# A hybrid convolution trunk on one core: activations stored as even then odd tokens and read alternately by TensorE, with VectorE's background tasks in smaller portions

## The chip, the cores and the metric

The kernel runs on one core of one Trainium2 chip. The metric is the device time of one execution in microseconds. Three timed runs of the kernel before gave 2077.26, 2077.28 and 2077.67 us; the median is 2077.28 us. Engines are named as in the profile: PE is TensorE's matmuls, PEld its weight loads, DVE is VectorE, ACT is ScalarE, POOL is GpSimd and SP is SyncE, which issues nearly all DMAs.

## What is computed

One layer of a decoder trunk for 320 tokens, 256 of one prompt and 64 of eight sampled sequences with eight tokens each, in float32, with 2048 channels:

```python
h = rmsnorm(x) * norm_mix_g
b_a, c_a, v_a, glu_a, glu_b, gate_a, gate_b = split(h @ w_in)
y_a = (b_a * causal_dwconv3(c_a * v_a)) @ w_out_a
u   = glu_a * sigmoid(glu_b)
z   = silu(layernorm(causal_dwconv31(u) + bias))
y_b = z @ w_out_b
x   = x + (sigmoid(gate_a) * y_a + sigmoid(gate_b) * y_b) @ w_o
h2  = rmsnorm(x) * norm_ffn_g
x   = x + (silu(h2 @ w_gate) * (h2 @ w_up)) @ w_down
y   = rmsnorm(x) * final_norm_g
```

The inner width of the last pair of products is 5632. The two convolutions run along the tokens of each sequence, and for the sampled sequences they continue from a stored state.

## The kernel before

**Layout.** Activations lie transposed: channels on the 128 partitions and the 320 tokens along the free dimension, one tile of 128x320 for each block of 128 channels. The host has laid out `x` in this way, with the gains of the first norm in front of it.

**Products.** Each float32 product is made of three matmuls on numbers split into a high part (`float32r`) and the remainder: high weight by high activation (L221), high weight by low activation (L222), low weight by high activation (L223). The weights are the stationary operand, 128x128, and the 320 tokens are the moving operand, which is read from one tile in the order of the tokens. A unit is a product that gives 256 output channels (`begin`, `run`): two accumulators in PSUM, and for each of its 128-channel steps three matmuls for each accumulator. Its weights come in pieces of four steps: 512 KB loaded on SP's queue (L146, five buffers, four pieces ahead), then the high part is cast by ACT (L181) and the remainder is subtracted by DVE (L185), two pieces ahead, into one of three pairs of buffers. A full piece is 24 matmuls.

**Order of the work.** The first three units run as one group while `x` arrives. Then come the units of the gated unit's two halves (`post_gb`, `post_ga`), of the three-tap mixer (`post_c`, `post_v`, `post_b`), of gate a and `w_out_a`, of gate b, of `w_out_b`, of `w_o`, then two halves of gate, up and down. Each unit ends in its `post` function, where DVE and ACT read the accumulators. Where the result is the next product's activation, `hilo` (L267) splits it: an ACT copy gives the high part and a DVE subtraction the low part. The high and low parts of the tiles `a`, `z`, `m` and `f` come from there, those of `g` from L582 and L583.

**Background tasks.** The 31-tap convolution of mixer B, and the layernorm after it, are lists of small tasks in `bg`, mostly for DVE (a tap is L394). After each piece `pump` takes tasks off the list until their written costs reach a budget; what a task took too much is carried over as debt. A tap's written cost is 0.42, a channel's end 0.4. The budgets are 0.9 in the first three units after the group, `BG1` = 1.3 for the ten units of the gated unit's rest (40 pieces), `BG2` = 1.3 for the 24 units of the three-tap mixer (96 pieces), and `BG3` = 1.1 for the units of the two gates and `w_out_a` (96 pieces). What is left is run at once before the units of `w_out_b`. The whole program passes through a scheduler that may move instructions within an engine's queue.

**The end.** The last 256 output channels of the last product are computed with tokens as rows (`run_rows`): there the activations are the stationary operand and 256 columns of weights the moving one, in 176 matmuls. Three blocks of tokens (`blk`: two of 128 of the prompt, one of the 64 sampled) are finished in turn by `Out`, which scales the rows, multiplies the tiles `xg` by the spread factors and writes them out. The norm's sums come from `row_sums`, as PE transposes of `facc`.

**Twenty matmuls more.** After the last block's DMAs have been put in the queue (L764 to L774), 20 matmuls write an accumulator that nobody reads. All have the same stationary tile. In order: four read a tile `v` of 128x320 in its order, four read it as `v.rearrange("p (a b) -> p b a", a=2)`, which takes word 0, word 160, word 1, word 161 and so on, four read 316 of its words from the third on, four read one word 320 times, and four read the same bytes as bfloat16.

Of the kernel before, what the change touches and what calls it, by code (L numbers as in the profile page):

```python
# [8 lines left out]
F32 = mybir.dt.float32  # L9
F32R = mybir.dt.float32r  # L10
I32 = mybir.dt.int32
AF = mybir.ActivationFunctionType
# [26 lines left out]
def trunk_kernel(ctx: ExitStack, tc: tile.TileContext, a):  # L39
# [22 lines left out]

    blk = [(0, P), (P, P), (2 * P, TS)]
    HD = D // 2
# [5 lines left out]
    gmix, xc[0] = lead[:, 0:NC], lead[:, NC : NC + T]  # L70
    sp.dma_start(out=lead, in_=a["x"][:, 0 : NC + T])

    def xcol(c):
        return a["x"][:, NC + c * T : NC + (c + 1) * T]

    def load_x(cs):
        for c in cs:
            xc[c] = slot("xc")
            sp.dma_start(out=xc[c], in_=xcol(c))  # L79

# [130 lines left out]
    def begin(u):  # L211
        acc = [ps_acc.tile([P, 512], F32, tag="acc", name=nm("acc")) for _ in range(u["nj"])]
        hi, lo = u["acts"]()
        nk = u["nk"]

        def prod(q, k, j):
            kk = q["ka"] + k
            wh = q["hi"][:, k, j * P : (j + 1) * P]
            wl = q["lo"][:, k, j * P : (j + 1) * P]
            o = acc[j][:, :T]  # L220
            te.matmul(o, wh, hi[kk], start=(kk == 0), stop=False)  # L221
            te.matmul(o, wh, lo[kk], start=False, stop=False)  # L222
            return te.matmul(o, wl, hi[kk], start=False, stop=(kk == nk - 1)).ins  # L223

        return acc, prod
# [64 lines left out]

    def sums(p, **kw):

        te.matmul(p[:, :T], ones_r, s_hi, start=True, stop=False)
        return te.matmul(p[:, :T], ones_r, s_lo, start=False, stop=True).ins

# [33 lines left out]
    def x_factor():  # L329
        p = pst("rps")  # L330
        halves(lnacc)
        with tc.issue_after(last_mm[0]):
            last_mm[0] = sums(p)
# [6 lines left out]
        ve.scalar_tensor_tensor(out=rb, in0=lnt, scalar=1.5, in1=rb, op0=ALU.add, op1=ALU.mult)  # L340

    def x_norm(c):
        hr = slot("hr")
        ve.scalar_tensor_tensor(out=hr, in0=xc[c], scalar=g_mix(c), in1=rb, op0=ALU.mult, op1=ALU.mult)
        h_hi[c], h_lo[c] = hilo(hr, "h")

# [225 lines left out]
    def post_o(b):  # L572
        def f(acc):
            for j in range(2):
                c = 2 * b + j
                xr = slot("xr")
                nc.sync.dma_start(out=xr, in_=xcol(c))
# [43 lines left out]
    def post_d1(b):  # L621
        def f(acc):
            for j in range(2):
                c = 2 * b + j
                ve.tensor_tensor(out=x2[c], in0=acc[j][:, :T], in1=x2[c], op=ALU.add)
        return f
# [36 lines left out]
    def pack(k):  # L663

        if k % 2 == 0:
            pk.append(slot("pk", F32R))
        t = pk[k // 2]
        ac.copy(out=t[:, (k % 2) * P : (k % 2) * P + TS], in_=f_hi[HF + k][:, TP:T])
        ac.copy(out=t[:, (k % 2) * P + TS : (k % 2 + 1) * P], in_=f_lo[HF + k][:, TP:T])

    def end_prep(n):

        if n == 0:
            t = slot("gfin", shape=(P, NB))
            nc.sync.dma_start(out=t, in_=a["final_norm_g"][CT * P : D].partition_broadcast(P))
            ve.tensor_scalar(out=t, in0=t, scalar1=-0.5, scalar2=None, op0=ALU.mult)
            gfin.append(t)
            for c in (CT, CT + 1):
                z = slot("xz", shape=(P, P))
                nc.gpsimd.memset(z[:, TS:P], 0.0)  # L680
                ac.copy(out=z[:, 0:TS], in_=x2[c][:, TP:T])
                xz.append(z)

    def run_rows(u):
        acc = [ps_acc.tile([P, 512], F32, tag="acc", name=nm("acc")) for _ in range(3)]

        def block(i, q, ks=None):
            for k in ks or range(q["n"]):
                kk = q["ka"] + k
                h, l, o = f_hi[HF + kk], f_lo[HF + kk], acc[i][:, :NB]  # L690
                wh, wl = q["hi"][:, k, :], q["lo"][:, k, :]
                t0 = blk[i][0]
# [69 lines left out]
        B.part(4, CB)  # L762


        o = ps_acc.tile([P, 512], F32, tag="acc", name=nm("acc"))
        w, v = f_hi[HF][:, 0:P], f_hi[HF + 1]
        wb, vb = f_hi[HF][:, 0 : P // 2].bitcast(mybir.dt.bfloat16), f_hi[HF + 1].bitcast(mybir.dt.bfloat16)
        with tc.issue_after(last_mm[0]):
            for rhs in (v, v.rearrange("p (a b) -> p b a", a=2), v[:, 2:318], v[:, 0:1].broadcast_to((P, T))):
                for _ in range(4):  # L770
                    r = o[:, : rhs.free_size()]
                    last_mm[0] = te.matmul(r, w, rhs, start=True, stop=True, skip_group_check=True).ins  # L772
            for _ in range(4):
                last_mm[0] = te.matmul(o[:, :T], wb, vb[:, 0:T], start=True, stop=True, skip_group_check=True).ins  # L774
    def row_sums():
        p = pst("pv")
        for i, (t0, n) in enumerate(blk):
            last_mm[0] = te.matmul(
                p[:n, i * P : (i + 1) * P], facc[:, t0 : t0 + n], ident, is_transpose=True, start=(i == 0), stop=True,
                skip_group_check=True,  # L780
            ).ins
# [8 lines left out]
    class Out:  # L790
# [77 lines left out]
        def part(self, c0, c1, eng=nc.sync):  # L868
            n, w = self.n, 1024 // self.n
            while c0 < c1:  # L870
                h = c0 * n // 1024
                e = min(c1, 12 if c0 < 12 else CT, (h + 1) * w)
                if self.out[h] is None:
                    self.out[h] = wp.tile([P, KP * NB], F32, tag="raw", bufs=RAW_BUFS, name=nm("yo"))
                o = self.out[h][:, (c0 - h * w) * n : (e - h * w) * n]
                t, k = (xgt[0], c0) if c0 < 12 else (xgt[1], c0 - 12)
                v = t[:, k * T : (k + e - c0) * T].rearrange("p (c t) -> p c t", t=T)[:, :, self.t0 : self.t0 + n]
                self.dve(
                    ve.tensor_tensor, out=o.rearrange("p (c t) -> p c t", t=n), in0=v,
                    in1=self.rb.unsqueeze(1).broadcast_to((P, e - c0, n)), op=ALU.mult,  # L880
                )
                eng.dma_start(out=self.dst[1][:, c0:e, :], in_=o)
# [51 lines left out]

    BG1, BG2, BG3 = 1.3, 1.3, 1.1
    first_units = group([
# [91 lines left out]


def _lay_in(np, i):  # L1030

# [5 lines left out]
    x = np.concatenate([f["x_prompt"].reshape(TP, D), f["x_sample"].reshape(TS, D)])  # L1037
    o["x"] = np.concatenate([_rows(np, f["norm_mix_g"]).reshape(P, NC), _rows(np, x).reshape(P, NC * T)], axis=1)
    names = ("final_norm_g", "norm_ffn_g", "conv_b_bias", "ln_b_g", "ln_b_b", "conv_a_w", "conv_b_w")
# [9 lines left out]
def _lay_out(np, y):  # L1049
    def rows(v, n):  # L1050
# [9 lines left out]
    return (  # L1060
        np.concatenate(yb[:2])[None],
        yb[2].reshape(SB, SS, D),
        np.ascontiguousarray(na[: WA - 1])[None, None],
# [24 lines left out]
```

## Time and profile before

| quantity | value |
|---|---|
| median of three timed runs | 2077.28 us |
| time of the profiled execution | 2076.96 us |
| its span, first to last instruction | 2075.2 us |
| PE busy, matmuls | 2069.2 us, 14117 |
| DVE busy | 1268.7 us (61%) |
| ACT busy | 807.7 us (39%) |
| DMA moved | 321.17 MB, 155 GB/s on average |
| granted TensorE clock | 1.000 |

The profiled execution lies 0.32 us under the median of the timed runs, and its own time 1.8 us over its span. Busy PE is no proof of a PE at its best, because matmuls are pipelined and their ends are modelled: a matmul of 320 columns shows 309 ns, though 14117 of them share 2069.2 us, 147 ns each. What counts is the distance from start to start. An engine's share over the whole span is an average of stages that differ, so the stages are read one by one.

### The profile page before, as it was taken

To read this page: it belongs to the slowest core of one execution; us is meant where nothing else is said; L and a number is where in the kernel's file an instruction comes from. 1 tells how busy PE (TensorE), PEld (TensorE's weight loads), DVE (VectorE), ACT (ScalarE), POOL (GpSimd) and SP (SyncE) were. 2 spreads that over 40 slices of the span, in tenths; PEclk is the share of its full clock that TensorE was granted. 3 is DMA by queue.
4 is the path that set the end of the run, shared out by engine and by line. 5 is a ranking of instruction groups with operands and counts; after the bars stand their busy time and mean duration, and the time that the engine had idled before them with its cause. 6 is when DMAs were issued, how large, how long until landed. Compare 5 with 4: busy or idle time off the path is not lost.

```text
span 2075.2 us, 33945 instructions
## 1 busy us (share of the span) xinstructions
PE 2069.2 (100%) x14117; PEld 2066.8 (100%) x14117; DVE 1268.7 (61%) x1854; ACT 807.7 (39%) x1172; POOL 4.5 (0%) x26
## 2 busy tenths in 40 slices
PE   9999999999999999999999999999999999999999
PEld 9999999999999999999999999999999999999999
DVE  7898889988986754345555645445334545545445
ACT  6544344444434344333344333333323333333433
POOL 0000000000000000000000000000000000000000
PEclk9999999999999999999999999999999999999999
DMA  7555544444444444444455444444455444444553
GB/s 268 156 171 156 181 145 153 153 149 147 155 153 145 150 153 149 148 151 153 151 174 173 152 146 150 153 150 141 146 159 152 148 151 153 148 148 147 150 153 112
DMA packets 97906, 321.17 MB, mean 155 GB/s; under 512 B 12920, under 2 KB 20920, under 8 KB 97720
## 3 DMA queue, kind: packets, MB, share of 16 engines
q1 hardware_dynamic: 97320, 318.48, 49.5%
q8 instruction: 110, 1.80, 0.4%
q10 hardware_dynamic: 432, 0.52, 0.1%
q14 instruction: 44, 0.36, 0.1%
HBM read 315.42 MB, written 4.98 MB: 154 GB/s over the span
## 4 chain that ended last, share of the span: by engine, by line
PE 99%; DMA 1%; DVE 0%; SPq 0%; ACT 0%; issue 0%
PE acc L223 33%; PE acc L221 33%; PE acc L222 33%; DMA raw<-in_w_in 1%; PE acc L695 0%; PE acc L696 0%; PE acc L697 0%; PE acc L700 0%; PE acc L701 0%; PE acc L772 0%; DVE yo L808 0%; DVE rl L320 0%; DVE wlo L185 0%; SPq L146 0%; SPq L79 0%; PE acc L708 0%
## 5 line engine op out<-in xcount | busy, mean ns | idle before, releaser
L185 DVE TENSOR_TENSOR wlo<-raw,whi 128x1024 fp32r<-128x1024 f32 (+1 forms) x602 | 717.3, 1192 | 706.5 <-ACT whi L181 703.5
L181 ACT CAST whi<-raw 128x1024 fp32r<-128x1024 f32 (+2 forms) x601 | 615.9, 1025 | 1177.6 <-PE acc L222 927.6
L222 PE MATMUL acc<-hl,whi 128*128 128x320 f32 x1600 | 494.2, 309 | 0.0
L221 PE MATMUL acc<-hh,whi 128*128 128x320 f32 x1600 | 493.8, 309 | 0.0
L223 PE MATMUL acc<-hh,wlo 128*128 128x320 f32 x1600 | 493.4, 309 | 0.0
L223 PE MATMUL acc<-gh,wlo 128*128 128x320 f32 x1408 | 435.1, 309 | 0.0
L222 PE MATMUL acc<-gl,whi 128*128 128x320 f32 x1408 | 435.1, 309 | 0.0
L221 PE MATMUL acc<-gh,whi 128*128 128x320 f32 x1408 | 435.1, 309 | 0.0
L222 PEld LDWEIGHTS acc<-hl,whi 128*128 128x128 f32 x1600 | 300.4, 188 | 0.0
L221 PEld LDWEIGHTS acc<-hh,whi 128*128 128x128 f32 x1600 | 300.3, 188 | 0.0
L223 PEld LDWEIGHTS acc<-hh,wlo 128*128 128x128 f32 x1600 | 300.2, 188 | 0.0
L221 PEld LDWEIGHTS acc<-gh,whi 128*128 128x128 f32 x1408 | 264.3, 188 | 0.0
L223 PEld LDWEIGHTS acc<-gh,wlo 128*128 128x128 f32 x1408 | 264.3, 188 | 0.0
L222 PEld LDWEIGHTS acc<-gl,whi 128*128 128x128 f32 x1408 | 264.3, 188 | 0.0
L394 DVE SCALAR_TENSOR_TENSOR cb<-win,prm,cb 128x320 f32<-128x320 f32 x480 | 257.2, 548 | 7.4
L221 PE MATMUL acc<-fh,whi 128*128 128x320 f32 x660 | 203.9, 309 | 0.0
L222 PE MATMUL acc<-fl,whi 128*128 128x320 f32 x660 | 203.9, 309 | 0.0
L223 PE MATMUL acc<-fh,wlo 128*128 128x320 f32 x660 | 203.9, 309 | 0.0
L222 PEld LDWEIGHTS acc<-fl,whi 128*128 128x128 f32 x660 | 123.9, 188 | 0.0
L223 PEld LDWEIGHTS acc<-fh,wlo 128*128 128x128 f32 x660 | 123.9, 188 | 0.0
L221 PEld LDWEIGHTS acc<-fh,whi 128*128 128x128 f32 x660 | 123.9, 188 | 0.0
L221 PE MATMUL acc<-ah,whi 128*128 128x320 f32 x256 | 79.1, 309 | 0.0
(183 smaller groups left out, 2039.2 us busy)
## 6 DMA issues: line engine op xcount, KB each, us to landing
raw<-in_w_in SPq DMA_DIRECT2D x221, 512.0 KB, 3.6
raw<-in_w_gate SPq DMA_DIRECT2D x88, 512.0 KB, 3.6
raw<-in_w_up SPq DMA_DIRECT2D x88, 512.0 KB, 3.6
raw<-in_w_down SPq DMA_DIRECT2D x80, 512.0 KB, 3.6
raw<-in_w_out_a SPq DMA_DIRECT2D x32, 512.0 KB, 3.6
raw<-in_w_out_b SPq DMA_DIRECT2D x32, 512.0 KB, 3.6
raw<-in_w_o SPq DMA_DIRECT2D x32, 512.0 KB, 3.7
raw<-in_w_down SPq DMA_DIRECT2D x16, 256.0 KB, 2.7
```

The costliest lines, as they stand in the source:

```text
L181: return f(out=q["hi"][:, ks, :], in_=q["raw"][:, ks, :]).ins
L185: return ve.tensor_tensor(out=q["lo"][:, ks, :], in0=q["raw"][:, ks, :], in1=q["hi"][:, ks, :].bitcast(F32), op=ALU.subtract).ins
L221: te.matmul(o, wh, hi[kk], start=(kk == 0), stop=False)
L222: te.matmul(o, wh, lo[kk], start=False, stop=False)
L223: return te.matmul(o, wl, hi[kk], start=False, stop=(kk == nk - 1)).ins
L394: ve.scalar_tensor_tensor(out=o, in0=win[0][:, :, j + 2 : j + 10], scalar=w_cb(j, c), in1=o, op0=ALU.mult, op1=ALU.add)
```

## The change

Tiles that PE streams are stored in halves: first the 160 even tokens, then the 160 odd ones. PE reads them with the pattern "p (a b) -> p b a", that is, one word from the first half and one from the second in turn, so the products come out in the order of the tokens as before. `alt` names this view of a stored tile, `seq2` the matching view of a tile in the order of tokens.

- `begin`: all three matmuls of each product read `alt(hi)` and `alt(lo)`.
- `hilo`, `post_o`, and the residual of the last product (`post_d2`, and `post_d1` for the last two channel blocks) write `alt` views from `seq2` views: on DVE and ACT the stored side then hops 160 words with each word. In the instructions these tiles stand as 128x160x2.
- The host stores a copy of `x` in halves (`xs`), which the first stage uses, so that `x_norm` stays in the stored order; it needs the norm's factors in that order as well, a copy `rbh` made once. `post_o` still loads `x` in the order of tokens.
- `run_rows`: the 256 weight columns of the last block of `w_down` are stored in halves by the host for its second half of rows, and read alternately. The blocks of tokens become even prompt tokens, odd prompt tokens and the sampled ones, which now are two runs of 32 in a tile (`smp`, `two`); the host puts the tokens of the output in order. `row_sums` first collects the sampled tokens' sums in a tile `fs` by an ACT copy.
- The 20 matmuls at the end are gone.
- `BG1` and `BG2` are 1.1 for 1.3, `BG3` is 1.25 for 1.1.

```diff
-    blk = [(0, P), (P, P), (2 * P, TS)]
+    HT = T // 2
+    blk = [(0, P), (HT, P), (P, TS)]
+    def alt(t):
+        return t.rearrange("p (a b) -> p b a", a=2)
+    def seq2(t):
+        return t.rearrange("p (b a) -> p b a", a=2)
+    def smp(t):
+        return t.rearrange("p (a b) -> p a b", a=2)[:, :, P:HT]
+    def two(t):
+        return t.rearrange("p (a b) -> p a b", a=2)
...
+        hi_, lo_ = lambda k: alt(hi[k]), lambda k: alt(lo[k])
...
-            te.matmul(o, wh, hi[kk], start=(kk == 0), stop=False)
-            te.matmul(o, wh, lo[kk], start=False, stop=False)
-            return te.matmul(o, wl, hi[kk], start=False, stop=(kk == nk - 1)).ins
+            te.matmul(o, wh, hi_(kk), start=(kk == 0), stop=False)
+            te.matmul(o, wh, lo_(kk), start=False, stop=False)
+            return te.matmul(o, wl, hi_(kk), start=False, stop=(kk == nk - 1)).ins
...
-    def hilo(val, s):
+    def hilo(val, s, halved=False):
+        ho, vi = (lambda t: t, lambda t: t) if halved else (alt, seq2)
...
-        ac.copy(out=h, in_=val)
-        ve.tensor_tensor(out=l, in0=val, in1=h.bitcast(F32), op=ALU.subtract)
+        ac.copy(out=ho(h), in_=vi(val))
+        ve.tensor_tensor(out=ho(l), in0=vi(val), in1=ho(h.bitcast(F32)), op=ALU.subtract)
...
+        rbh.append(slot("rbh"))
+        ve.tensor_copy(out=alt(rbh[0]), in_=seq2(rb))
...
-        ve.scalar_tensor_tensor(out=hr, in0=xc[c], scalar=g_mix(c), in1=rb, op0=ALU.mult, op1=ALU.mult)
-        h_hi[c], h_lo[c] = hilo(hr, "h")
+        ve.scalar_tensor_tensor(out=hr, in0=xc[c], scalar=g_mix(c), in1=rbh[0], op0=ALU.mult, op1=ALU.mult)
+        h_hi[c], h_lo[c] = hilo(hr, "h", True)
...
-                ac.activation(out=h, in_=x2[c], func=AF.Copy, scale=g_ffn(c))
-                ve.scalar_tensor_tensor(out=l, in0=x2[c], scalar=g_ffn(c), in1=h.bitcast(F32), op0=ALU.mult, op1=ALU.subtract)
+                ac.activation(out=alt(h), in_=seq2(x2[c]), func=AF.Copy, scale=g_ffn(c))
+                ve.scalar_tensor_tensor(
+                    out=alt(l), in0=seq2(x2[c]), scalar=g_ffn(c), in1=alt(h.bitcast(F32)), op0=ALU.mult, op1=ALU.subtract
+                )
...
-                x3 = x2[c]
-                ve.tensor_tensor(out=x3, in0=acc[j][:, :T], in1=x3, op=ALU.add)
+                x3 = slot("x3")
+                ve.tensor_tensor(out=alt(x3), in0=seq2(acc[j][:, :T]), in1=seq2(x2[c]), op=ALU.add)
...
-                wh, wl = q["hi"][:, k, :], q["lo"][:, k, :]
+                wh, wl = alt(q["hi"][:, k, :]), alt(q["lo"][:, k, :])
...
-        with tc.issue_after(last_mm[0]):
-            for rhs in (v, v.rearrange("p (a b) -> p b a", a=2), v[:, 2:318], v[:, 0:1].broadcast_to((P, T))):
...
+        fs = slot("fs", shape=(P, TS))
+        ac.copy(out=two(fs), in_=smp(facc))
...
-    BG1, BG2, BG3 = 1.3, 1.3, 1.1
+    BG1, BG2, BG3 = 1.1, 1.1, 1.25
```

Two places show what moves on DVE. The first lies early among the units of gate a and `w_out_a`, around the products of the first such unit (`ma`). The rows `wlo` are the splits of the weights, `cb` the taps of one channel block of the convolution. Before:

```order
L300 TENSOR_TENSOR lnacc<-lnacc,cb_6204 128x320
L185 TENSOR_TENSOR wlo_6558<-raw_6489,whi_6557 128x1024
L554 TENSOR_TENSOR ma_6587<-acc_6455,gt_6451 128x320
L554 TENSOR_TENSOR ma_6589<-acc_6456,gt_6453 128x320
L185 TENSOR_TENSOR wlo_6596<-raw_6522,whi_6595 128x1024
L394 SCALAR_TENSOR_TENSOR cb_6630<-win_370,prm,cb_6630 128x320 x4
L185 TENSOR_TENSOR wlo_6638<-raw_6555,whi_6637 128x1024
L394 SCALAR_TENSOR_TENSOR cb_6630<-win_370,prm,cb_6630 128x320 x4
```

The same place after the change, with the line numbers of the changed kernel:

```order
L319 TENSOR_TENSOR lnacc<-lnacc,cb_6156 128x320
L200 TENSOR_TENSOR wlo_6480<-raw_6411,whi_6479 128x1024
L417 SCALAR_TENSOR_TENSOR cb_6516<-win_370,prm,cb_6516 128x320
L577 TENSOR_TENSOR ma_6519<-acc_6376,gt_6372 128x320
L577 TENSOR_TENSOR ma_6521<-acc_6377,gt_6374 128x320
L417 SCALAR_TENSOR_TENSOR cb_6516<-win_370,prm,cb_6516 128x320
L200 TENSOR_TENSOR wlo_6528<-raw_6444,whi_6527 128x1024
L417 SCALAR_TENSOR_TENSOR cb_6516<-win_370,prm,cb_6516 128x320 x4
L200 TENSOR_TENSOR wlo_6560<-raw_6477,whi_6559 128x1024
```

In the kernel before, DVE is here at the last channel block of the convolution; in the changed one two more blocks are still to come after this one, so that taps which stood among the earlier units now stand among these.

The second place is the end of a unit of `post_b` in the three-tap mixer, where DVE multiplies (`av`) and splits (`al`) the activations of `w_out_a`. Before:

```order
L485 TENSOR_TENSOR av_4037<-acc_3894,ca_3876 128x320
L394 SCALAR_TENSOR_TENSOR cb_3933<-win_370,prm,cb_3933 128x320 x2
L185 TENSOR_TENSOR wlo_4054<-raw_3971,whi_4053 128x1024
L271 TENSOR_TENSOR al_4040<-av_4037,ah_4039 128x320
L485 TENSOR_TENSOR av_4043<-acc_3895,ca_3888 128x320
L394 SCALAR_TENSOR_TENSOR cb_3933<-win_370,prm,cb_3933 128x320 x2
L185 TENSOR_TENSOR wlo_4087<-raw_4004,whi_4086 128x1024
L271 TENSOR_TENSOR al_4046<-av_4043,ah_4045 128x320
```

And after:

```order
L508 TENSOR_TENSOR av_4440<-acc_4299,ca_4281 128x320
L417 SCALAR_TENSOR_TENSOR cb_4371<-win_370,prm,cb_4371 128x320 x2
L200 TENSOR_TENSOR wlo_4457<-raw_4375,whi_4456 128x1024
L289 TENSOR_TENSOR al_4443<-av_4440,ah_4442 128x160x2
L508 TENSOR_TENSOR av_4446<-acc_4300,ca_4293 128x320
L417 SCALAR_TENSOR_TENSOR cb_4371<-win_370,prm,cb_4371 128x320 x2
L200 TENSOR_TENSOR wlo_4490<-raw_4407,whi_4489 128x1024
L289 TENSOR_TENSOR al_4449<-av_4446,ah_4448 128x160x2
```

The order around the split of the activations is the same; only its form is new, 128x160x2.

More of the change, by code (lines that the diff above doesn't have):

```diff
@@ L70, in trunk_kernel @@
     gmix, xc[0] = lead[:, 0:NC], lead[:, NC : NC + T]
-    sp.dma_start(out=lead, in_=a["x"][:, 0 : NC + T])
-    def xcol(c):
-        return a["x"][:, NC + c * T : NC + (c + 1) * T]
+    sp.dma_start(out=lead, in_=a["xs"][:, 0 : NC + T])
     def load_x(cs):
@@ L78, in load_x @@
             xc[c] = slot("xc")
-            sp.dma_start(out=xc[c], in_=xcol(c))
+            sp.dma_start(out=xc[c], in_=a["xs"][:, NC + c * T : NC + (c + 1) * T])
     idle = slot("idle", F32R)
@@ L289, in halves, with sums @@
         ve.tensor_tensor(out=s_lo, in0=v, in1=s_hi.bitcast(F32), op=ALU.subtract)
-    def sums(p, **kw):
-        te.matmul(p[:, :T], ones_r, s_hi, start=True, stop=False)
-        return te.matmul(p[:, :T], ones_r, s_lo, start=False, stop=True).ins
+    def sums(p, halved=False):
+        f = alt if halved else lambda t: t
+        te.matmul(p[:, :T], ones_r, f(s_hi), start=True, stop=False)
+        return te.matmul(p[:, :T], ones_r, f(s_lo), start=False, stop=True).ins
     def csum(dst, src, c):
@@ L624, in f @@
                 c = 2 * b + j
-                ve.tensor_tensor(out=x2[c], in0=acc[j][:, :T], in1=x2[c], op=ALU.add)
+                o = x2[c]
+                if c < CT:
+                    ve.tensor_tensor(out=o, in0=acc[j][:, :T], in1=o, op=ALU.add)
+                else:
+                    x2[c] = slot("x3")
+                    ve.tensor_tensor(out=alt(x2[c]), in0=seq2(acc[j][:, :T]), in1=seq2(o), op=ALU.add)
         return f
@@ L667, in pack @@
         t = pk[k // 2]
-        ac.copy(out=t[:, (k % 2) * P : (k % 2) * P + TS], in_=f_hi[HF + k][:, TP:T])
-        ac.copy(out=t[:, (k % 2) * P + TS : (k % 2 + 1) * P], in_=f_lo[HF + k][:, TP:T])
+        ac.copy(out=two(t[:, (k % 2) * P : (k % 2) * P + TS]), in_=smp(f_hi[HF + k]))
+        ac.copy(out=two(t[:, (k % 2) * P + TS : (k % 2 + 1) * P]), in_=smp(f_lo[HF + k]))
     def end_prep(n):
@@ L680, in end_prep @@
                 nc.gpsimd.memset(z[:, TS:P], 0.0)
-                ac.copy(out=z[:, 0:TS], in_=x2[c][:, TP:T])
+                ac.copy(out=two(z[:, 0:TS]), in_=smp(x2[c]))
                 xz.append(z)
@@ L762, in run_rows @@
         B.part(4, CB)
-        o = ps_acc.tile([P, 512], F32, tag="acc", name=nm("acc"))
-        w, v = f_hi[HF][:, 0:P], f_hi[HF + 1]
-        wb, vb = f_hi[HF][:, 0 : P // 2].bitcast(mybir.dt.bfloat16), f_hi[HF + 1].bitcast(mybir.dt.bfloat16)
-        with tc.issue_after(last_mm[0]):
-            for rhs in (v, v.rearrange("p (a b) -> p b a", a=2), v[:, 2:318], v[:, 0:1].broadcast_to((P, T))):
[L770 to L774, printed above, removed]
     def row_sums():
         p = pst("pv")
+        fs = slot("fs", shape=(P, TS))
+        ac.copy(out=two(fs), in_=smp(facc))
         for i, (t0, n) in enumerate(blk):
+            v = fs if i == 2 else facc[:, t0 : t0 + n]
             last_mm[0] = te.matmul(
-                p[:n, i * P : (i + 1) * P], facc[:, t0 : t0 + n], ident, is_transpose=True, start=(i == 0), stop=True,
+                p[:n, i * P : (i + 1) * P], v, ident, is_transpose=True, start=(i == 0), stop=True,
                 skip_group_check=True,
```

31 lines of the change are left out of this document (21 added, 10 removed).

## The prediction

> **What bounds the kernel now.** The page comes first: busy shares, the granted clock, and the chain that ended last.
>
> ```profile
> PE 2069.2 (100%) x14117; PEld 2066.8 (100%) x14117; DVE 1268.7 (61%) x1854; ACT 807.7 (39%) x1172; POOL 4.5 (0%) x26
> PEclk9999999999999999999999999999999999999999
> PE 99%; DMA 1%; DVE 0%; SPq 0%; ACT 0%; issue 0%
> PE acc L223 33%; PE acc L221 33%; PE acc L222 33%; DMA raw<-in_w_in 1%; PE acc L695 0%; PE acc L696 0%; PE acc L697 0%; PE acc L700 0%; PE acc L701 0%; PE acc L772 0%; DVE yo L808 0%; DVE rl L320 0%; DVE wlo L185 0%; SPq L146 0%; SPq L79 0%; PE acc L708 0%
> ```
>
> PE is 99% of the chain, at full granted clock, in the three matmul lines of the units. Next, the windows by stage (columns: window, its length, then busy us and instructions of PE, PEld, DVE, ACT, POOL; clock, DMA share, GB/s) and the list of waits of PE and of the splits.
>
> ```profile
> 4.50:18.80 14.30, 13.02 (x77) 11.85 (x76) 10.91 (x27) 10.66 (x26) 0.00 (x0) 1.00 0.97 313
> 18.80:30.00 11.20, 11.18 (x76) 11.18 (x77) 11.16 (x19) 10.07 (x20) 0.00 (x0) 1.00 1.03 384
> 50.30:571.30 521.00, 521.00 (x3555) 521.00 (x3554) 460.12 (x758) 228.48 (x384) 2.88 (x14) 1.00 0.51 157
> 571.30:797.10 225.80, 225.80 (x1541) 225.80 (x1541) 151.22 (x231) 89.22 (x117) 0.00 (x0) 1.00 0.48 150
> 797.10:2045.30 1248.20, 1248.20 (x8513) 1248.19 (x8512) 603.24 (x762) 449.00 (x591) 0.30 (x2) 1.00 0.50 152
> ```
>
> ```profile
> PE spin L86 <- DVE idle L83: 1.3, 1, 1.3
> PE rbp L838 <- DVE rst L808: 1.0, 1, 1.0
> PE acc L221 <- ACT whi L181: 0.9, 1, 0.9
> PE acc L223 <- DVE wlo L185: 0.2, 1, 0.2
> ...
> ACT whi L181 <- PE acc L222: 927.6, 402, 2.9
> DVE wlo L185 <- ACT whi L181: 703.5, 461, 3.4
> ```
>
> In the long last stage 1248.20 us for 8513 matmuls are 146.6 ns from start to start. PE waits for its weights for 1.1 us in all; ACT's casts wait for PE 927.6 us (for a buffer), and DVE's subtractions for the casts. So the suppliers run ahead of PE, and the time is the number of matmuls times their pitch. Any change of the pitch is multiplied by about 13,800.
>
> **The pitch after the change.** The kernel before has the new reading pattern in it: four of the 20 matmuls at its end (the probe) read alternately. The timeline of PE, asked in narrow windows (start, us from there, how many), gives:
>
> ```profile
> 2069.88 0.60 PE L772 MATMUL acc<-fh,fh 128*128 128x320 f32 x3
> 2070.03 0.59 PE L772 MATMUL acc<-fh,fh 128*128 128x320 f32 x3
> 2070.32 0.71 PE L772 MATMUL acc<-fh,fh 128*128 128x320 f32 x4
> 2070.73 0.73 PE L772 MATMUL acc<-fh,fh 128*128 128x320 f32 x4
> 2070.86 0.45 PE L772 MATMUL acc<-fh,fh 128*128 128x316 f32 x2
> 2072.00 0.72 PE L774 MATMUL acc<-fh,fh 128*128 128x320 bf16 x4
> ```
>
> The second matmul in order starts at 2069.88, the first alternating one at 2070.32: 0.44 us for three, 146.7 ns each, the pitch of the stream. The fourth alternating one starts at 2070.73, 0.41 us for three (136.7), and the first of 316 words at 2070.86, 0.54 us for four (135.0). Starts are rounded to 10 ns, so the alternating pitch lies between 135.0 and 136.7; I take 135.6, in the middle of that and of the durations:
>
> ```profile
> L772 PE MATMUL acc<-fh,fh 128*128 128x320 f32 x2 | 0.4, 299 | 0.0
> L222 PE MATMUL acc<-hl,whi 128*128 128x320 f32 x1600 | 494.2, 309 | 0.0
> L222 PEld LDWEIGHTS acc<-hl,whi 128*128 128x128 f32 x1600 | 300.4, 188 | 0.0
> L772 PEld LDWEIGHTS acc<-fh,fh 128*128 128x128 f32 x5 | 0.7, 188 | 0.0
> ```
>
> Two alternating matmuls alone show 299 ns, those of the stream 309: 10 ns less, as the starts have it. Each of the probe's matmuls has a weight load of 188 ns as in the stream, and the tile and the hop of 160 words are those of the change. The Trainium skill, "TensorE: Matmul & The Clock Gate", section Back-to-back issue gap, gives N / 2.4 + 2.5 ns, an estimate of 135.8 for 320 columns; the alternating read agrees, the ordered one (146.6) does not.
>
> One rule speaks against the change. The Trainium skill, "Advanced Engine Details and Errata", section SBUF Cachelines, says that at least two hits on a 16-byte line are needed to absorb the access latency, and that a different line with each access is penalized. By it the alternating read would be the slower one; the starts above say the opposite, for four matmuls. It stays as a rival.
>
> **Part by part.** *Units.* The products have 3 x 4628 = 13,884 matmuls of 320 columns: 14,117 less 11 at the start, 20 in the probe, 176 in `run_rows` and 26 for sums, transposes and spreads. The 77 before 18.8 us wait for the first loads and splits and gain nothing. 13,807 x (146.6 - 135.6) = 151.9 us.
>
> *Rows.* The 176 matmuls of 256 columns, in the same proportion, gain 8.8 ns each: 1.5 us. No row shows an alternating read of 256 with a hop of 128; the bounds are this gain and as much loss. I take the gain, since the 320-column row is the nearest.
>
> *Start.* From 18.8 to 30.0 DVE is busy 11.16 of 11.20 us and cannot go faster with PE. At worst the share of those 11.2 us is not gained, 0.8 us; I charge it.
>
> *The split views on DVE.* 124 operations of 320 words (108 splits, 16 residual sums) and `rbh` hop with every word. No row shows such a hop on DVE or ACT. Below:
>
> ```profile
> L394 DVE SCALAR_TENSOR_TENSOR cb<-win,prm,cb 128x320 f32<-128x320 f32 x480 | 257.2, 548 | 7.4
> L344 DVE SCALAR_TENSOR_TENSOR hr<-xc,lead,rb 128x320 f32<-128x320 f32 x15 | 8.2, 544 | 0.0
> L185 DVE TENSOR_TENSOR wlo<-raw,whi 128x1024 fp32r<-128x1024 f32 x572 | 700.3, 1224 | 674.4 <-ACT whi L181 671.5 <-DMA raw<-in_w_in 0.3
> L185 DVE TENSOR_TENSOR wlo<-raw,whi 128x512 fp32r<-128x512 f32 x18 | 12.4, 691 | 30.1 <-ACT whi L181 30.1
> ```
>
> The taps read runs of eight words and cost what a read in order does (548 against 544), so the low end is nothing; a gain is excluded, as the words are as many. For the high end I double the cost of a word: (1224 - 691) / 512 = 1.04 ns, so 0.33 us each. Runs of one are far from runs of eight, so I take 0.2 us: 25 us in all, of which 17 operations, 3.4 us, lie before 571 us. The Trainium skill, "Vector Engine (DVE) Microarchitecture Reference", section Measured stream behaviour on trn2, has 1.98 against 1.054 ns per column with all three streams hopping, an estimate of 0.30 us for each, 37 us in all. On ACT, busy 44% at most in the three stages from 50.3 us on, twice the cost would still be covered.
>
> *The budgets.* 0.2 less over 40 + 96 pieces, at 0.42 a tap, moves 65 taps out of 50-571 us; at 257.2 / 480 = 0.536 us each that is 34.8 us. There DVE then has 460.1 - 34.8 + 3.4 = 428.7 us to do while PE takes 521.0 x 135.6 / 146.6 = 481.9: 89%, against 88% before, when PE did not wait. In 571-797 us it has 151.2 + 34.8 = 186.0 of 208.9: 89%, against 67%, with some of its tail passing to the stage behind. After that DVE has 603.2 + 22 of 1154.5 us: 54%. So what is late next is DVE before 797 us, but it stays within what it can do on average; for single pile-ups, such as the layernorm's chain in front of a split, I charge 0.5 us, between 0 and 2. Without the budgets the first share would be 463.5 / 481.9 = 96%.
>
> *DMA.* 0.50 of the engines' time at 146.6 becomes 0.54 at 135.6. Nothing.
>
> *The waits that are added.* The copy `fs` stands in ACT's queue behind a weight cast and ahead of two others; behind it wait only casts that are due two pieces later, and PE's three transposes, for which two pieces of matmuls are the cover: nothing. The copy `rbh` is DVE work like L344's 0.54 us, with 0.33 more at most, ahead of the first `hr`; the first unit that reads `h` comes three units later: nothing.
>
> *The end.* The chain's last entry is the probe, but the last output's DMA is issued beside it and lands later:
>
> ```profile
> 2070.69 0.89 SPq L882 DMA_DIRECT2D out_y<-yo x2
> ...
> out_y<-yo SPq DMA_DIRECT2D x5, 256.0 KB, 2.6
> ```
>
> The second issue ends at 2071.58, and some 2.6 us from issue to landing lead past the probe's end, 2072.00 + 0.72. Removing the probe gives 0.
>
> The sum: 151.9 + 1.5 - 0.8 - 0.5 = 152.1 us off the profiled execution's 2076.96 us, 1924.9; the median of the runs lay 0.3 us above that execution. Forecast 1925 us, 7.3% less.
>
> **The rivals.**
>
> *DVE becomes the bound before 797 us.* The windows of two short stretches:
>
> ```profile
> 70.00:80.00 10.00, 10.00 (x70) 10.00 (x70) 9.50 (x19) 4.35 (x7) 0.00 (x0) 1.00 0.55 153
> 80.00:92.60 12.60, 12.60 (x88) 12.60 (x87) 11.59 (x21) 5.29 (x9) 0.00 (x0) 1.00 0.54 170
> ```
>
> For it: in these 22.6 us DVE is busy 21.09, which is 101% of 20.9, and hops have an unknown price. Against it: the stage as a whole keeps its share, and the same rows show PE without a gap. If neither stage got shorter, 746.8 x 0.075 = 56 us would be kept back: 1981 us. In milder forms half of it: 1953. Chance 0.06.
>
> *The change does not do what it says in the stream.* The probe's four matmuls share one stationary tile, the stream's change it each time; if that, not the order of words, sets 146.6 ns, nothing is gained and DVE's 25 us stay covered: 2077 us. Against it: the probe's four matmuls in order share it too and have 146.7. Chance 0.03.
>
> *Slower.* The alternating read pays for its lines once PE streams it for milliseconds while ACT, DVE and the weight loads write the same memory, more than in the quiet end. Each ns of pitch is 13.8 us, and it decides from 146.6 ns on. As far above as the probe is below, 157.6 ns, it would be 2077 + 152 = 2229 us. For it: only four in a row were seen, and no loads of weights beside them. Against it: the starts, with PE's own weight loads in between. By the rule on lines in the Trainium skill's "Advanced Engine Details and Errata" this would be the expected result. Chance 0.04.
>
> **How the numbers follow.** The forecast has 0.87. Low end: pitch 135.0, no charges, 2077.3 - 160.2 - 1.5 = 1915. High end: pitch 136.7, 136.7 us, rows losing 1.5, the start 0.8 and pile-ups 2: 1945. The range leaves out two rivals and most of the first. Faster by over 0.2% (4 us, about what the measurement can tell from no change) is the forecast and DVE's bound: 0.93; within 0.2%: 0.03; slower: 0.04.
>
> **What would show it.** Matmuls of L221 to L223 at 299 ns and, in a window of the last stage, 135 to 136 ns each; PE still 99% of the chain; the DVE row of 128x160x2 forms between 0.48 and 0.82 us; DVE near 89% in both early stages and PE waits under 3 us. A pitch above 137 in the last stage, where DVE is half idle, would refute the probe's transfer; a good pitch there and a long one before 797 us would mean that DVE binds.

## The result and the profile after

The changed kernel takes 1927.1 us (median of 4 runs, 1926.94 to 1927.36) against 2077.27 us (4 runs, 2077.12 to 2077.67). The ratio is 0.9277, with a 95% interval of 0.9261 to 0.9293. The forecast was 1925, with a range of 1915 to 1945.

The page of the kernel after, with the shares of the engines, the granted clock, the chain that ended last by engine, and one group of the stream:

```profile
span 1925.5 us, 33924 instructions
PE 1916.0 (100%) x14097; PEld 1914.0 (99%) x14097; DVE 1288.1 (67%) x1855; ACT 834.9 (43%) x1173; POOL 4.4 (0%) x26
PEclk9999999999999999999999999999999999999999
PE 98%; DMA 1%; DVE 1%; issue 0%; ACT 0%; SPq 0%; DVEq 0%
L238 PE MATMUL acc<-hl,whi 128*128 128x320 f32 x1600 | 478.3, 299 | 0.0
```

The span is 149.7 us shorter, the same work by fewer nanoseconds: the matmuls of the units show 299 ns where they showed 309, as the four alternating ones of the probe did. PE still carries 98% of the chain. The windows of the kernel after, with the columns as before, for the stretches that answer to 50.3-571.3, 571.3-797.1, 797.1-2045.3 and the end of the kernel before:

```profile
49.00:531.50 482.50, 482.50 (x3552) 482.50 (x3553) 431.26 (x696) 227.49 (x372) 2.46 (x12) 1.00 0.54 169
531.50:741.00 209.50, 209.48 (x1542) 209.24 (x1541) 176.44 (x282) 90.59 (x124) 0.41 (x2) 1.00 0.52 161
741.00:1896.80 1155.80, 1155.80 (x8511) 1155.80 (x8510) 626.34 (x774) 476.33 (x597) 0.30 (x2) 1.00 0.53 164
1896.80:1925.50 28.70, 22.42 (x197) 21.83 (x195) 16.88 (x40) 8.61 (x19) 0.00 (x0) 0.92 0.26 93
```

The end of the kernel before, in the same columns:

```profile
2045.30:2075.20 29.90, 26.45 (x215) 25.54 (x213) 16.35 (x40) 8.34 (x18) 0.00 (x0) 0.99 0.25 88
```

In the long stage 1155.80 us for 8511 matmuls are 135.8 ns each, against 146.6. DVE is busy 89% of the first stretch, 84% of the second and 54% of the third, and PE waits for 4.2 us in all. Its waits in the kernel after (total us, times, longest):

```profile
PE spin L101 <- DVE idle L98: 1.2, 1, 1.2
PE rbp L859 <- DVE rst L829: 1.0, 1, 1.0
PE acc L237 <- ACT whi L196: 0.9, 1, 0.9
PE acc L237 <- ACT rh L338: 0.6, 1, 0.6
PE acc L239 <- DVE wlo L200: 0.3, 1, 0.3
PE acc L237 <- DVE sg L434: 0.2, 1, 0.2
```

What the change costs stands in the groups by form. Each of these operations had 484 ns on DVE and 455 on ACT for `f`, and 546 on DVE for `g`:

```profile
L288 ACT CAST fh<-ft 128x320 fp32r<-128x320 f32 x44 | 30.5, 801 | 0.0
L289 DVE TENSOR_TENSOR fl<-ft,fh 128x320 fp32r<-128x320 f32 x44 | 29.0, 739 | 0.0
L606 DVE SCALAR_TENSOR_TENSOR gl<-x,prm,gh 128x320 fp32r<-128x320 f32 x16 | 12.7, 792 | 0.0
```

The profile writes the new form as 128x320 too. An operation whose stored side hops with every word takes 0.25 us longer on DVE and 0.35 on ACT. That this is hidden behind PE is shown by the last experiment.

### The profile page after: what moved, and what is told of

Read it like the earlier page. It is cut to its first block, busy times and chain, and to the rows that moved or that the text cites. A ratio compares the mean times of both kernels' runs of the same rounds, so it can differ in the third digit from the quotient of the medians.

```text
span 1925.5 us, 33924 instructions
## 1 busy us (share of the span) xinstructions
PE 1916.0 (100%) x14097; PEld 1914.0 (99%) x14097; DVE 1288.1 (67%) x1855; ACT 834.9 (43%) x1173; POOL 4.4 (0%) x26
## 4 chain that ended last, share of the span: by engine, by line
PE 98%; DMA 1%; DVE 1%; issue 0%; ACT 0%; SPq 0%; DVEq 0%
PE acc L239 32%; PE acc L237 32%; PE acc L238 32%; DMA raw<-in_w_in 1%; PE acc L725 0%; DVE wlo L200 0%; PE acc L726 0%; PE acc L727 0%; DVE yo L829 0%; PE acc L731 0%; PE acc L730 0%; ACT whi L196 0%; DVE rl L339 0%; SPq L161 0%; SPq L94 0%
## 5 line engine op out<-in xcount | busy, mean ns | idle before, releaser
L238 PE MATMUL acc<-hl,whi 128*128 128x320 f32 x1600 | 478.3, 299 | 0.0
L237 PE MATMUL acc<-hh,whi 128*128 128x320 f32 x1600 | 477.7, 299 | 0.0
L239 PE MATMUL acc<-hh,wlo 128*128 128x320 f32 x1600 | 477.7, 299 | 0.0
L237 PE MATMUL acc<-gh,whi 128*128 128x320 f32 x1408 | 421.3, 299 | 0.0
L239 PE MATMUL acc<-gh,wlo 128*128 128x320 f32 x1408 | 421.3, 299 | 0.0
L238 PE MATMUL acc<-gl,whi 128*128 128x320 f32 x1408 | 421.2, 299 | 0.0
L239 PE MATMUL acc<-fh,wlo 128*128 128x320 f32 x660 | 197.5, 299 | 0.0
L237 PE MATMUL acc<-fh,whi 128*128 128x320 f32 x660 | 197.5, 299 | 0.0
L238 PE MATMUL acc<-fl,whi 128*128 128x320 f32 x660 | 197.5, 299 | 0.0
L238 PE MATMUL acc<-zl,whi 128*128 128x320 f32 x256 | 76.6, 299 | 0.0
```

Of the source, the lines that this page charges most:

```text
L237: te.matmul(o, wh, hi_(kk), start=(kk == 0), stop=False)
L238: te.matmul(o, wh, lo_(kk), start=False, stop=False)
L239: return te.matmul(o, wl, hi_(kk), start=False, stop=(kk == nk - 1)).ins
```

## The experiments

Each kernel was run on the same chip as the kernel before, whose median was 2077.0 to 2077.1 us there. The two kernels on reading orders and lengths were run once each.

**The reading undone.** The changed kernel, whose units read the stored halves straight through:

```diff
-        hi_, lo_ = lambda k: alt(hi[k]), lambda k: alt(lo[k])
+        hi_, lo_ = lambda k: hi[k], lambda k: lo[k]
```

> The changed kernel with one thing undone: the matmuls of the units read their stored tiles straight through, word after word, instead of alternately. Everything else of the change stays (halved storage with its hopping writes, budgets, no probe). The products then come out with their tokens in stored order, so the convolutions mix other tokens and the output is not the reference's; the work is as much. Theory (the gain is the pitch of the alternating read alone): 13,807 matmuls x (146.67 - 135.83) = 149.7 us come back, 1927.1 + 149.7 = 2076.8 us, matmuls at 309 ns, PE still without waits. Rival (halved storage, the smaller budgets or the missing probe bring a part of it): clearly below 2070 us.

Measured: 2076.04 us, ratio to the kernel before 0.9995 (0.9986 to 1.0004). Its page, one group of the stream and one of the splits:

```profile
PE 2064.9 (100%) x14097; PEld 2063.0 (99%) x14097; DVE 1301.1 (63%) x1855; ACT 839.1 (40%) x1173; POOL 4.5 (0%) x26
L238 PE MATMUL acc<-hl,whi 128*128 128x320 f32 x1600 | 494.1, 309 | 0.0
L289 DVE TENSOR_TENSOR fl<-ft,fh 128x320 fp32r<-128x320 f32 x44 | 29.8, 764 | 0.0
```

The matmuls are back at 309 ns with everything else of the change in place, the slower splits included. So the gain is the order in which the moving operand is read. This run lies 1.0 us under the kernel before, which its interval does not tell from nothing; its 176 matmuls of the rows still read alternately.

**The old budgets in the new kernel.**

```diff
-    BG1, BG2, BG3 = 1.1, 1.1, 1.25
+    BG1, BG2, BG3 = 1.3, 1.3, 1.1
```

> The changed kernel with the budgets of before (1.3, 1.3, 1.1). Theory (DVE has room enough, and the splits' two pieces of lead carry it over pile-ups): DVE busy about 464 of 482.5 us in the stretch from 49 to 531 us, 96%, and the time within 2 us of 1927.1. Rival (DVE becomes the bound there, and only the new budgets keep the gain): PE waits for the weights' low parts in many pieces before 531 us, and the time is 1935 to 1960 us.

Measured: 1927.26 us, ratio 0.9279 (0.9266 to 0.9291), the time of the changed kernel. Its first stretch:

```profile
49.00:531.50 482.50, 482.50 (x3553) 482.50 (x3554) 455.05 (x758) 231.95 (x386) 2.87 (x14) 1.00 0.55 169
```

DVE has 455.05 of 482.5 us to do, 94% where 96% was expected, and PE goes on without a gap. The new budgets were not needed for the gain.

**The new budgets in the kernel before.** The same line the other way round.

> The kernel before with the new budgets (1.1, 1.1, 1.25) alone. Theory: PE waits for nothing before and after, 2077.3 us within 0.5. Rival (the budgets carry a part of the 150 us): below 2073 us.

Measured: 2076.97 us, ratio 1.0 (0.9991 to 1.0008). Nothing, as expected: it moved 60 taps and 25.5 us of DVE's busy time out of the first stretch (434.67 us there for 460.12) into the second, and PE's time did not change.

**Large budgets.** To find the load at which DVE takes over:

```diff
-    BG1, BG2, BG3 = 1.1, 1.1, 1.25
+    BG1, BG2, BG3 = 1.8, 1.8, 1.1
```

> The changed kernel with BG1 and BG2 at 1.8 for 1.1 and BG3 at 1.1. It puts 109 taps more, 109 x 0.54 = 58 us of DVE, into the stretch that took 482.5 us with 431.3 us of DVE: 490 us of work, 101%, and about 107% in its first quarter. Theory (DVE binds once its work exceeds PE's time, not before): PE waits for the low parts of the weights for 10 to 30 us in all, time 1937 to 1957 us, and the stages behind are as before. Rival (the scheduler's order and the lead of two pieces absorb it): 1927 to 1930 us.

Measured: 1927.18 us, ratio 0.9277 (0.9261 to 0.9292). The theory missed, and its rival was right. The windows show by how much the sum was off. The last two rows are the taps alone on DVE in this stretch, first in the changed kernel, then in this run:

```profile
88.20:218.60 130.40, 130.40 (x962) 130.40 (x961) 130.10 (x227) 60.28 (x93) 1.02 (x5) 1.00 0.58 179
49.00:531.50 482.50, 482.28 (x3551) 482.07 (x3550) 462.78 (x814) 233.72 (x387) 2.86 (x14) 1.00 0.55 169
...
49.00:531.50 482.50, 200.81 (x369) 1.00 0.54 169
49.00:531.50 482.50, 243.34 (x480) 1.00 0.55 169
```

There are 111 taps more (109 were reckoned with), and DVE's busy time rose by 462.78 - 431.26 = 31.5 us where 58 were expected. That is 0.28 us for each tap more, but it is not the price of a tap: the taps by themselves rose by 42.5 us, and all 480 of them take 0.51 us each where the 369 took 0.54. Four taps in a row (start, us), first in the changed kernel, then in this run, show what differs:

```profile
123.18 2.31 DVE L417 SCALAR_TENSOR_TENSOR cb<-win,prm,cb 128x320 f32<-128x320 f32 x4
124.25 1.94 DVE L417 SCALAR_TENSOR_TENSOR cb<-win,prm,cb 128x320 f32<-128x320 f32 x4
```

A tap shows 0.55 us in both. There the taps begin (2.31 - 0.55) / 3 = 0.59 us apart, here 0.46, so that one begins before the one before it has ended and busy time does not add up from means. What makes the taps follow each other more closely here is not shown. And in the stretch with DVE at 130.10 of 130.40 us PE stands not once: a DVE that hardly pauses did not hold PE up.

**Each tap twice.**

```diff
+            if not twin:
+                twin.append(slot("twin"))
+            o_ = twin[0].rearrange("p (g t) -> p g t", t=SS)
+            ve.scalar_tensor_tensor(out=o_, in0=win[0][:, :, j + 2 : j + 10], scalar=w_cb(j, c), in1=o, op0=ALU.mult, op1=ALU.add)
```

> The changed kernel with each of the 480 taps made twice on DVE, the second time into a tile that nobody reads. Work is added, none is left out. It asks at which load DVE takes over from PE. DVE had 431.3 + 176.4 = 607.7 us to do in the 692 us from 49 to 741 us; 480 more taps cost 0.31 us each by what a tap added in the run with large budgets (13.0 us for 42) or 0.54 by the tap's busy time, 149 to 259 us. That makes 757 to 867 us, 109 to 125% of PE's time. Theory (DVE binds when its work exceeds PE's time): 65 to 175 us longer, 1992 to 2102 us, with PE waiting for low parts of weights and for the layernorm. Rival (the large lead and the room after 741 us take it up): below 1950 us.

Measured: 2132.56 us, ratio to the kernel before 1.0267 (1.0252 to 1.0282), 205 us above the changed kernel. DVE binds, as the theory has it, but the size is past its high end, and the place is another. The page's slices of PE, DVE and the clock, PE's wait for the weights' low parts, and two matmuls with the time that PE stood before them:

```profile
PE   9999999999999100099999999999999999999998
DVE  7999999999999999995465665555544455555555
PEclk9999999999999655599999999999999999999999
...
PE acc L239 <- DVE wlo L200: 0.6, 2, 0.3
...
897.66 0.63 PE L312 MATMUL mu<-s_hi,ones_r 128*128 128x320 f32 x1 [196.93 <-ACT s_hi L306]
902.83 0.64 PE L237 MATMUL acc<-ah,whi 128*128 128x320 f32 x1 [4.01 <-ACT gt L574]
```

PE hardly waits for the weights' low parts (0.6 us). It waits once for long, 196.9 us, at the matmul that makes the layernorm's mean: that one needs every tap of all channels, and everything behind it in PE's queue waits with it. Of the rest, 4.0 us are the wait right behind it, and the matmuls that follow start 0.27 us apart (903.52, 903.79, 904.05) until 906.18 us, after a wait in which the clock was granted at about half.

Two terms of the sum were off. It counted room until 741 us, but PE comes to the matmul of the mean at about 700.7 us and needs all the taps there. And the low price was wrong: DVE's busy time on the page rose by 1542.0 - 1288.1 = 253.9 us, 0.53 us for each tap more. In the changed kernel the low part of that sum is done at 654.9 us and the matmul comes at 665.17: 10.3 us in hand. That is no fixed room. The matmul is itself an entry of `bg` behind the taps, so the written costs and the budgets set its place; with the large budgets the sum is done at 499.0 us and the matmul comes at 538.56. The second tap has no written cost, so `pump` handed out twice the work at the same rate.

**Reading orders.** The changed kernel with 288 matmuls more at its end, 16 to an order, here two of them:

```diff
+            for _ in range(16): mm(v, T)
+            for _ in range(16): mm(alt(v), T)
```

> The changed kernel with 18 times 16 more matmuls at its end whose result nobody reads, all with one stationary tile, each group with another order of reading the moving operand: straight, halves word by word (hop 160), halves in pairs of words, in fours, swaps inside small groups (second word 2, 4, 8, 16, 32 words away), every second and every third word of a longer tile, and straight against halves for 512, 128 and 256 columns. Theory A (a straight read pays because neighbouring words are read one after the other from the same line, so any order without neighbours is fast): word by word at any distance of 4 words or more, and every second word or third, at 135.8 ns; pairs and fours nearer to 146.7. Theory B (what counts is that two far regions are read in turn): only hops of many words are fast, strides and small swaps at 146.7 or slower. Straight reads cost 10% of their columns by either: 512 columns 234.7 against 215.8 ns, 256 columns 117.3 against 109.2, 128 columns 58.7 against 55.8.

The orders stood in the sequence in which the expectation names them, then 316 words from the second on. The timeline of PE in one window for each (start, us, how many); N matmuls take N pitches and 0.163 us, so the first row is (2.21 - 0.163) / 14 = 146.2 ns:

```profile
1919.91 2.21 PE L798 MATMUL acc<-fh,fh 128*128 128x320 f32 x14
1922.37 1.93 PE L798 MATMUL acc<-fh,fh 128*128 128x320 f32 x13
1924.48 3.17 PE L798 MATMUL acc<-fh,fh 128*128 128x320 f32 x14
1928.01 2.16 PE L798 MATMUL acc<-fh,fh 128*128 128x320 f32 x13
1930.45 2.07 PE L798 MATMUL acc<-fh,fh 128*128 128x320 f32 x13
1932.77 1.93 PE L798 MATMUL acc<-fh,fh 128*128 128x320 f32 x13
...
1941.47 4.25 PE L798 MATMUL acc<-whi,fh 128*128 128x320 f32 x14
...
1950.60 3.34 PE L798 MATMUL acc<-whi,fh 128*128 128x512 f32 x14
1954.22 3.19 PE L798 MATMUL acc<-whi,fh 128*128 128x512 f32 x14
...
1961.27 1.72 PE L798 MATMUL acc<-fh,fh 128*128 128x256 f32 x13
1963.17 1.61 PE L798 MATMUL acc<-fh,fh 128*128 128x256 f32 x13
```

Row by row: straight 146.2; halves word by word 135.9; halves in pairs 214.8; in fours 153.6; swaps within four words 146.7; swaps within eight (hop of four words) 135.9, and the same for hops of 8, 16 and 32 in the rows left out. Every second word of a long tile takes 291.9, every third 284.8 (a row left out). Theory A holds for the hops and fails for the strides and the pairs; theory B fails at the hop of four. Word by word from two places is fast at every distance tried here from four words on, all of them multiples of four, which is 16 bytes; no other order of these words is. At 512 columns straight costs 226.9 against 216.2: the surcharge is 10.7 ns again, not a tenth. At 256 it is 119.8 against 111.3, and at 128, in rows left out, both take 111, where 58.7 and 55.8 were expected.

The probe of the kernel before has two more reads that bear on this. The first row holds the four matmuls that read one word 320 times, the second three that read the bytes straight as bfloat16:

```profile
2071.45 0.71 PE L772 MATMUL acc<-fh,fh 128*128 128x320 f32 x4
2072.15 0.57 PE L774 MATMUL acc<-fh,fh 128*128 128x320 bf16 x3
```

The first bfloat16 matmul starts at 2072.00, so the four of one word took 0.55 us, about 138 ns each: reading the same word again, in the same place, is not slow. The straight bfloat16 read, with half the bytes, takes (0.57 - 0.163) / 3 = 135.7. So not every straight read pays the surcharge; with words of four bytes it does.

**Lengths and the weight load.** Thirteen more orders in the same way, among them:

```diff
+            for _ in range(16): mm(v, T, f_hi[HF][:, 0:1].broadcast_to((P, P)))
+            for _ in range(16): mm(v, T, f_hi[HF][:, 0:256:2])
```

> The changed kernel with 13 times 16 other matmuls at its end that nobody reads. In the first such run a straight read cost 10.8 ns over an alternating one at 320 columns and the same 10.8 at 512, against 10% of the columns expected. Theory C (a straight read pays once for each matmul): the difference at 288, 384 and 448 columns is 10.8 ns each time, and the alternating ones are N / 2.4 + 2.5, 122.5, 162.5 and 189.2 ns. Rival (it grows with the columns): 9.8, 13.0 and 15.2 ns. Theory D (the straight read is held up by the weight load beside it): with a stationary tile of one word read 128 times, the straight read of 320 falls to 135.8; with a stationary tile of every second word it rises above 146.7. Rival: 146.7 in both. Quarters, eighths and sixteenths read in turn and a hop of five words: 135.8 if it is enough that neighbours in time lie in different 16-byte lines and the next reads come back to them.

The timeline in windows: the two stationary tiles above, 384 columns straight (all, then the last eight of them) and alternating, 288 likewise, then quarters word by word and a hop of five words:

```profile
1919.86 2.20 PE L798 MATMUL acc<-fh,fh 128*128 128x320 f32 x14
1922.34 2.07 PE L798 MATMUL acc<-fh,fh 128*128 128x320 f32 x13
1924.56 2.61 PE L798 MATMUL acc<-whi,fh 128*128 128x384 f32 x14
1925.63 1.55 PE L798 MATMUL acc<-whi,fh 128*128 128x384 f32 x8
1927.51 2.27 PE L798 MATMUL acc<-whi,fh 128*128 128x384 f32 x13
...
1936.33 1.87 PE L798 MATMUL acc<-fh,fh 128*128 128x288 f32 x13
1938.41 1.75 PE L798 MATMUL acc<-fh,fh 128*128 128x288 f32 x13
1940.46 2.38 PE L798 MATMUL acc<-fh,fh 128*128 128x320 f32 x13
...
1947.53 2.17 PE L798 MATMUL acc<-fh,fh 128*128 128x320 f32 x13
```

The straight read stays at 145.5 and 146.7 ns whatever the weight load reads: theory D falls in the form in which it was put; a matmul with no weight load beside it was not run. The surcharge is 131.3 - 122.1 = 9.2 ns at 288 columns, 174.8 - 162.1 = 12.7 at 384 and, in rows left out, 202.6 - 189.1 = 13.5 at 448. That looks like growth, as the rival has it, but at 384 the first matmuls of the group were the slow ones: the last eight take (1.55 - 0.163) / 8 = 173.4 ns, 11.3 more than alternating, and 512 had only 10.7. So neither theory C nor the rival is borne out: the surcharge is 10.7 to 11.3 at 320, 384 and 512, less at 288 and more at 448. Quarters take 170.5, eighths 274.8 and sixteenths 312.6 (rows left out), a hop of five words 154.4: that neighbours in time lie in different lines and come back to them is not enough. Of the orders tried, those are fast that go word by word between two places a multiple of 16 bytes apart. What in the read path makes the surcharge stays open.

**A near hop in the stream.** The kernel before without its probe, tiles in the order of tokens, straight writes:

```diff
+        near = lambda t: t.rearrange("p (g a b) -> p g b a", a=2, b=4)
...
-            te.matmul(o, wh, hi[kk], start=(kk == 0), stop=False)
+            te.matmul(o, wh, near(hi[kk]), start=(kk == 0), stop=False)
```

> The kernel before, with its tiles stored in the order of tokens, without the probe, and with one edit: the matmuls of the units read alternately inside groups of eight words (word 0, 4, 1, 5, 2, 6, 3, 7). The products come out with their tokens in that order, so the convolutions mix other tokens and the output is not the reference's; the work is as much, and DVE and ACT write straight. Theory (what pays is that two neighbours in time lie in two lines; halves far apart, hopping writes and smaller budgets are not needed for the time): pitch 135.8 in the stream, 1927 us within 3. Rival (near hops collide when the rest of the chip writes the same memory, or the stream needs halves): matmuls above 299 ns, above 1940 us.

Measured: 1928.13 us, ratio 0.9283 (0.9267 to 0.9298). Its long stage and its end:

```profile
740.30:1896.10 1155.80, 1155.80 (x8511) 1155.80 (x8510) 601.99 (x762) 447.70 (x591) 0.30 (x2) 1.00 0.54 164
1896.10:1926.20 30.10, 23.82 (x197) 23.22 (x195) 16.70 (x40) 8.39 (x18) 0.00 (x0) 0.98 0.25 88
```

The long stage takes the same 1155.80 us for the same 8511 matmuls, with DVE 24 us and ACT 29 us less busy in it. So the stream needs no far halves. The whole run is 1.0 us longer than the changed kernel; its end, where the rows are still read straight, is 1.4 us longer. Up to a few tenths of a microsecond, then, the new storage with its slower splits neither adds to the time nor takes from it. None of these kernels is faster than the changed one.

## Why the prediction was right, step by step

*The units.* Forecast 151.9 us from a pitch of 135.6 ns, less 0.8 for the start and 0.5 for pile-ups, 150.6. Measured, stretch by stretch: 50.3 - 49.0 = 1.3 us at the start, 38.5, 16.3 and 92.4 in the three stretches, 148.5 in all. The probe's four matmuls held for all 13,884 of the stream, and the reading undone gave it all back. The 2.1 us that are missing are the pitch: 135.8 for 135.6, and 146.6 less that on 13,807 matmuls is 149.1 before any charge. The mechanism was right; how near the number came is in part luck. Starts rounded to 10 ns allow 0.40 to 0.42 us for three pitches and 0.53 to 0.55 for four, that is 133.3 to 137.5 ns and not the 135.0 to 136.7 of the range; at 137.5 the time would have been 13,807 x 1.7 = 23 us longer, outside the range.

The estimate of 135.8 from the Trainium skill's "TensorE: Matmul & The Clock Gate", section Back-to-back issue gap, was nearer than the middle that I took from the rows. But the page gives that formula for a single matmul by itself, and about 131 ns at 512 columns for a stream of weight loads and matmuls. The alternating matmuls here, each with its weight load, took 216.2 at 512: for these float32r operands the formula fits and the figure for the stream does not.

*The start and pile-ups.* From 18.8 to 50.3 us PE had 214 matmuls, which at 10.8 ns would save 2.3 us, and 1.3 came of it: the charge of 0.8 was about right. No pile-up shows before 531 us, and PE's waits for the weights' splits are 1.2 us in all for 1.1.

*The rows and the end.* Forecast 1.5 us for the rows, with as much loss possible, and nothing for the probe's removal. The stretch behind the last unit takes 28.7 us for 29.9. The added matmuls of 256 columns took 119.8 straight and 111.3 alternating, 176 x 8.5 = 1.5 us, so the rows explain the 1.2 us and nothing is left for the probe.

*The split views.* Forecast 0.2 us each on DVE between bounds of 0 and 0.33: measured 0.25. In all DVE's busy time rose by 1288.1 - 1268.7 = 19.4 us for 25, but that mixes in the budgets and the faster PE. With the new budgets and straight reads on both sides it is 1301.1 us with the new storage (the reading undone) and 1275.1 without it (the new budgets in the kernel before), 26.0 us. The Trainium skill's "Vector Engine (DVE) Microarchitecture Reference", section Measured stream behaviour on trn2, led to an estimate of 0.30, for all three streams hopping; in the splits two of the three hop. On ACT it is 0.35 of 0.46, less than twice, as assumed. As forecast, the time shows none of it: the near hop, without these costs, takes as long in the long stage.

*The budgets.* The shares came out as worked out in two of three stretches: 431.3 of 482.5 us (428.7 of 481.9 forecast), 626.3 of 1155.8 (625 of 1154.5); the second was 176.4 for 186.0. That the first came so near is luck, since two terms were too large and almost cancel: without the new budgets DVE had 455.05 us there and not 463.5, and the budgets took 455.05 - 431.26 = 23.8 us out of it and not 34.8. But the sentence that without the new budgets the first share would be 96% treated a share as if it neared a limit; 94% in the stretch, and 99.8% in a quarter of it with the large budgets, cost nothing.

*The rivals.* That DVE becomes the bound was refuted at the loads of this change; its price was sought in the wrong place too. Where DVE did bind, with each tap made twice, the price was not spread over the pieces but was one wait at the layernorm's mean. That nothing is gained in the stream, and that the stream is slower, fell with the pitch. The Trainium skill's rule on lines ("Advanced Engine Details and Errata", section SBUF Cachelines) is not borne out for the moving operand: a read that changes the line with each word, coming back to both lines, is the fastest of all that were tried (135.9 ns), and every second word, with two words used in each line one after the other, takes twice the time of a straight read (291.9 against 146.2).

## What to carry to other kernels

When one engine has no gaps, look for a cheaper form of its commonest instruction and measure that in a few instructions at the end of the kernel that exists: four matmuls forecast 150 us to within 2%, closer than their rounded starts could promise. Here a moving operand of float32r, read word by word from two places a multiple of 16 bytes apart, ran at 135.8 ns for 320 columns, and a straight one 8% slower. And do not read a helper engine's high share as a bound: ask which instruction of the bounding engine's queue is the first to need its last result, and how long before that it is ready.

## What the runs showed of the hardware that was not expected

- Orders that look kinder are far worse: pairs from two halves 214.8 ns for 320 words, every second word 291.9, eighths in turn 274.8, against 146.2 straight and 135.9 for single words from two places.
- The pitch has a floor: 128 and 256 columns, read alternately, both take 111 ns, and 128 read straight as well. Each of these matmuls loads 128 columns of weights; that this load sets the floor was not tested.
- Taps that each show 0.55 us on DVE began 0.46 us apart in one run and 0.59 in another. One more tap raised DVE's busy time by 0.28 us in the first of these runs and by 0.53 where each tap was made twice, so one run's price does not carry over to the next.
- While PE waited 197 us for the layernorm's mean, the granted clock fell to about half, and the first matmuls after the wait started 0.27 us apart; 8.5 us after the wait they were 0.136 apart again.
